# Rotary turning in a hybrid decoder trunk: one product and one sum of six operations put on GpSimd

## The chip, the core and the metric

The kernel runs on one core of a Trainium2 chip. The metric is the device time of one execution in microseconds (us). The engines are named as in the profile: PE (TensorE) multiplies matrices, DVE (VectorE) and ACT (ScalarE) work element by element, POOL (GpSimd) does a little arithmetic and issues a large part of the transfers, SP issues the loads of the weights.

## The reference, cut to what matters

Two layers are applied to 512 prompt positions and 8 sample positions at once, with a model width of 2048. Everything is in 32-bit floats.

```python
h = rmsnorm(x, norm_g)
z = h @ w_in                                   # 2048 x 8192
b_c, c_c, x_c, g_c, q, k, v, g_r = split_projection(z)
y_conv = b_c * short_conv(c_c * x_c) * silu(g_c)
q = rope(q.reshape(Bsz, L, 4, 256), pos)
k = rope(k.reshape(Bsz, L, 4, 256), pos) * 256 ** -0.5
o, new_S = retention(q, k, v, ret_S)           # four heads, chunks, state carried on
y_ret = groupnorm(o) * gn_g * silu(g_r)
x = x + concat(y_conv, y_ret) @ w_out
x = x + sigmoid(x @ w_pg) * (p_i @ w_ple)
```

`rope` splits each head of 256 into halves x1 and x2 and gives x1 cos - x2 sin and x1 sin + x2 cos: four products, one difference and one sum.

## The kernel before, in words

All activations lie with the features on the 128 partitions and the 520 positions (512 + 8) along the row, one slot of 128 x 520 floats for 128 features; there are 75 such slots in SBUF. A product of 2048 x 128 weights with all positions is computed twice over 260 columns (LEFT and RIGHT).

**Precision and the split.** Each float operand is cut into a high part and a remainder: ACT rounds to the high part (L229) and DVE subtracts it (L230). Each product is then three matmuls (L247 to L249): high by high, high by low, low by high. The weights come by SP's queue into a ring `raw` of 32 blocks of 128 x 128, and their parts go into a ring `split` of 60 blocks, from which PE reads. A block of a ring is free again only when its last reader is done.

**Pairs of products.** Two products at a time run through `pair`: for part of the depth (14 or 16 of the 16 blocks) by Strassen's method, which needs sums of weights, made by DVE in `raw` (L319), and the rest plainly. The finished halves are copied from PSUM to slots by ACT or added by DVE (L307 is the helper that records such operations with raised priority).

**A layer.** For each of four heads `retain(h)` takes q, k, v and the gate through `pair`. After q and after k it calls `rope`, copies the 8 sample positions to a small tile (`qks`, L830 and L839 on ACT), and stores the two turned slots to DRAM (`hs`, L815, a transfer issued by POOL). The chunks of retention are computed later, in nine steps (`steps`) that are put between the products of the next pairs; they fetch their pieces of q, k, v back from `hs` (L870, POOL). Then follow eight blocks of the convolution branch, the output product and the gate. Between pairs the states of the 8 samples are updated (`sample_step`): ACT scales (L777), DVE updates (L781) and reduces (L785), POOL loads and stores (L771, L772, L782).

**The turning.** `rope` has six operations on 128 x 520 slots. a and b are the two halves, rc and rs tables of cosine and sine that already hold the norm's factor, t1 and t2 fresh slots. L753 is t1 = a rc, L754 is t2 = a rs, L755 is a = b rs (it writes over a, so it must follow L753 and L754), L756 is t1 = t1 - a, L757 is b = b rc (after L755, which still reads b), and L758 is b = b + t2. There are 16 calls: q and k of four heads in two layers. In the profiled execution the calls of layer 0 lie between 69 and 345 us and those of layer 1 between 1117 and 1418 us.

**What sets the order.** The program is built by a framework whose scheduler, with a model of times of its own, sets for each engine one fixed order of instructions; each engine then works through its order without overtaking, and waits on semaphores where an operand is not ready. An instruction that waits therefore holds up everything behind it on its engine, POOL's transfers included.

Of the kernel before, what the change touches and what calls it, by code (L numbers as in the profile page):

```python
# [11 lines left out]
MUL, ADD, SUB = ALU.mult, ALU.add, ALU.subtract  # L12
# [67 lines left out]
class Slots:  # L80
# [8 lines left out]
    def get(self, dtype=F32):  # L89
        i = self.free.pop(0)  # L90
        self.count += 1
        t = self.pool.tile([P, T], dtype, tag=f"s{i}", name=f"slot{i}_{self.count}")
        self.used[id(t)] = (t, i)
        return t
# [4 lines left out]
    def put(self, *slots):  # L99
        for t in slots:  # L100
            self.free.append(self.used.pop(id(t))[1])
# [90 lines left out]
def trunk_kernel(  # L192
# [6 lines left out]
    V, S, G, PE, DMA = nc.vector, nc.scalar, nc.gpsimd, nc.tensor, nc.sync  # L199
# [516 lines left out]
    for l in range(DEPTH):  # L716
# [5 lines left out]
        def prepare():  # L722
            rc, rs = get(), get()
            SIDE.dma_start(rc, cosT)
            SIDE.dma_start(rs, sinT)
            with tc.high_priority():
                root = rms.root()
                rb = rms.spread(rms.diagonal(root))
                V.tensor_tensor(rc, rc, rb, MUL)
                V.tensor_tensor(rs, rs, rb, MUL)  # L730
            return root, rb, rc, rs

        def copied(ps):
            t = get()
            for n, v in zip((LEFT, RIGHT), ps):
                S.activation(t[:, n], v, AF.Copy)
            banks.put(*[v for v in ps if not any(v is o for o in over)])
            return Val(put, slot=t)
# [3 lines left out]
        root, rb, rc, rs = prepare()  # L742
# [6 lines left out]
        def rope(z0, z1):  # L749

            a, b = ((z if z.ps is None else copied(z.ps)).slot for z in (z0, z1))
            t1, t2 = get(), get()
            V.tensor_tensor(t1, a, rc, MUL)  # L753
            V.tensor_tensor(t2, a, rs, MUL)  # L754
            V.tensor_tensor(a, b, rs, MUL)  # L755
            V.tensor_tensor(t1, t1, a, SUB)  # L756
            V.tensor_tensor(b, b, rc, MUL)  # L757
            V.tensor_tensor(b, b, t2, ADD)  # L758
            put(a, t2)
            return [t1, b]  # L760

# [56 lines left out]
        def retain(h):  # L818
# [6 lines left out]
            if l == 0 and h == 0:  # L825
                q = rope(*first[:2])
            else:
                q = rope(*head(mt))
# [5 lines left out]
            if l == 0 and h == 0:  # L834
                kf = rope(*first[2:])
            else:
                kf = rope(*head(mt + 2))
# [641 lines left out]
```

## Time and profile before

| | |
|---|---|
| median of 3 runs | 2170.08 us (2166.74 to 2172.5) |
| profiled execution | 2172.46 us |
| its span | 2170.4 us, granted clock 0.998 |
| PE busy | 2148.5 us (99%), 17861 matmuls |
| DVE busy | 1895.7 us (87%) |
| ACT busy | 1266.2 us (58%) |
| POOL busy | 430.5 us (20%), 746 instructions |

The busy time of PE counts matmuls that overlap each other; whether PE runs at its pace is better read from the number of matmuls in equal stretches of time. "Idle before" and the view of waits name the instruction that ended a wait. "issue" is a wait for which the profile shows no cause.

### The profile page before, as it was taken

What the parts mean: (1) busy time and instruction counts of PE and PEld (TensorE: products, weight loads), DVE (VectorE), ACT (ScalarE), POOL (GpSimd) and SP (SyncE); (2) the same over time, 40 slices, a digit from 0 to 9 for tenths busy, and PEclk for the clock granted to TensorE, in tenths of its full rate; (3) what the DMA queues carried; (4) which work ended last, traced back from release to release, by engine and by line L of the source; (5) the groups of instructions that cost most, each with busy time, mean ns of one, the idle gap of its engine ahead of it and who ended that gap; (6) DMA issues with size and microseconds to landing.
All of it is one profiled execution on the core that took longest, in us unless ns stands there. A gap on an engine that the chain in (4) does not pass through costs nothing. (4 is left out here: it accounts for less than half of the span.)

```text
span 2170.4 us, 48198 instructions
## 1 busy us (share of the span) xinstructions
PE 2148.5 (99%) x17861; PEld 2142.9 (99%) x17861; DVE 1895.7 (87%) x3849; ACT 1266.2 (58%) x2661; POOL 430.5 (20%) x746
## 2 busy tenths in 40 slices
PE   9999999999999999999999999999999999999998
PEld 9999999999999999999999999999999999999998
DVE  8889989898999987987897988989999998878884
ACT  8656556655555555655765655565655555456565
POOL 2313222211001211210212222231111022121011
PEclk9999999999999999999999999999999999999999
DMA  8556675545543645645645566665464455566455
GB/s 288 176 169 196 185 215 183 186 152 172 156 134 120 228 156 186 217 153 161 214 144 174 172 210 193 190 195 183 147 182 145 127 155 199 181 212 195 127 169 192
DMA packets 182861, 387.31 MB, mean 178 GB/s; under 512 B 25888, under 2 KB 56352, under 8 KB 182624
## 3 DMA queue, kind: packets, MB, share of 16 engines
q1 hardware_dynamic: 129136, 213.77, 31.8%
q0 software_dynamic: 53056, 169.84, 23.8%
q8 instruction: 140, 2.29, 0.4%
q14 instruction: 97, 0.79, 0.1%
q10 hardware_dynamic: 432, 0.61, 0.1%
HBM read 318.96 MB, written 65.15 MB: 177 GB/s over the span
## 5 line engine op out<-in xcount | busy, mean ns | idle before, releaser
L247 PE MATMUL ps_g<-slot,split 128*128 128x260 f32 x5465 | 1532.3, 284 | 9.7 <-ACT slot L307 3.4
L248 PE MATMUL ps_g<-slot,split 128*128 128x260 f32 x5465 | 1535.1, 283 | 0.3 <-DVE slot L555 0.3
L249 PE MATMUL ps_g<-slot,split 128*128 128x260 f32 x5461 | 1520.5, 283 | 0.5 <-DVE split L230 0.5
L229 ACT ACTIVATE split<-raw 128x512 fp32r<-128x512 f32 (+2 forms) x1347 | 778.2, 596 | 587.6 <-DVE raw L319 205.6
L247 PEld LDWEIGHTS ps_g<-slot,split 128*128 128x128 f32 x5465 | 1024.5, 188 | 12.9 <-ACT slot L307 4.2
L248 PEld LDWEIGHTS ps_g<-slot,split 128*128 128x128 f32 x5465 | 1029.3, 188 | 0.5 <-DVE slot L555 0.5
L249 PEld LDWEIGHTS ps_g<-slot,split 128*128 128x128 f32 x5461 | 1020.3, 188 | 0.8 <-DVE split L230 0.7
L230 DVE TENSOR_TENSOR split<-raw,split 128x512 fp32r<-128x512 f32 (+2 forms) x1346 | 844.1, 647 | 176.5 <-PE ps_g L248 85.4
L319 DVE TENSOR_TENSOR raw<-raw 128x512 f32<-128x512 f32 (+1 forms) x660 | 426.2, 656 | 28.1 <-DMA raw<-wi 18.4
L307 ACT ACTIVATE slot<-ps_g 128x260 f32<-128x260 f32 x336 | 127.2, 381 | 142.5 <-PE ps_g L249 127.2
L551 ACT ACTIVATE slot<-slot 128x520 fp32r<-128x520 f32 (+1 forms) x212 | 109.1, 562 | 41.8 <-DVE slot L414 10.2
L552 DVE TENSOR_TENSOR slot<-slot,slot 128x520 fp32r<-128x520 f32 (+1 forms) x212 | 122.9, 609 | 4.3 <-ACT slot L551 4.2
L782 POOL DMA_DIRECT2D o_rets<-slot x64 | 35.3, 552 | 350.6 <-DVE slot L781 131.8
L307 DVE TENSOR_TENSOR slot<-ps_g,slot 128x260 f32<-128x260 f32 x168 | 70.5, 421 | 7.3 <-PE ps_g L249 4.9
L870 POOL DMA_DIRECT2D slot<-hs x64 | 46.1, 723 | 126.5 <-DVE split L230 35.5
L815 POOL DMA_DIRECT2D hs<-slot x64 | 35.6, 556 | 137.9 <-DVE slot L756 59.6
L747 DVE TENSOR_TENSOR slot<-slot,slot 128x520 f32<-128x520 f32 x80 | 55.4, 692 | 4.6 <-DMA o_rets<-slot 3.7
L1059 POOL DMA_DIRECT2D slot<-x1s x76 | 40.8, 538 | 88.0 <-PE ps_g L249 28.3
L781 DVE SCALAR_TENSOR_TENSOR slot<-slot,vs,slot 128x256 f32<-128x256 f32 x128 | 55.9, 477 | 2.6 <-ACT slot L777 2.3
L1209 POOL DMA_DIRECT2D x2s<-slot x30 | 16.3, 545 | 203.4 <-DVE slot L1204 202.5
L771 POOL DMA_DIRECT2D slot<-sret x64 | 35.5, 555 | 106.4 <-ACT split L229 43.4
L772 POOL DMA_DIRECT2D slot<-kq x64 | 34.9, 547 | 109.2 <-DVE slot L877 20.5
(217 smaller groups left out, 1727.0 us busy)
## 6 DMA issues: line engine op xcount, KB each, us to landing
raw<-wi SPq DMA_DIRECT2D x377, 256.0 KB, 3.9
raw<-wo SPq DMA_DIRECT2D x128, 256.0 KB, 5.6
raw<-wg SPq DMA_DIRECT2D x122, 256.0 KB, 4.2
raw<-wi SPq DMA_DIRECT2D x136, 192.0 KB, 4.0
slot<-x1s POOLq DMA_DIRECT2D x76, 260.0 KB, 5.0
slot<-sret POOLq DMA_DIRECT2D x64, 256.0 KB, 4.0
hs<-slot POOLq DMA_DIRECT2D x64, 256.0 KB, 3.9
slot<-hs POOLq DMA_DIRECT2D x64, 256.0 KB, 5.1
```

The source lines that it names most:

```text
L229: S.activation(hi, raw, AF.Copy)
L230: V.tensor_tensor(lo, raw, F(hi), SUB)
L247: PE.matmul(out, wh, xh, start=start, stop=False, skip_group_check=more)
L248: PE.matmul(out, wh, xl, start=False, stop=False, skip_group_check=more)
L249: PE.matmul(out, wl, xh, start=False, stop=stop, skip_group_check=more)
L307: fn(*args)
L319: V.tensor_tensor(out[:, n], x[:, n], y[:, n], op)
L551: keep(S.activation(hi, src[:, n], AF.Copy))
L552: V.tensor_tensor(lo, src[:, n], F(hi), SUB)
L747: V.tensor_tensor(out[:, n], v, table[:, n], MUL)
L781: keep(V.scalar_tensor_tensor(st[:, c], k, vs[:, h, e, b : b + 1], st[:, c], MUL, ADD))
L870: SIDE.dma_start(t[:, :512].rearrange("p (m n) -> p m n", m=2), src)
```

## The change

Two of the six operations of `rope` are given to POOL: the product a = b rs and the sum b = b + t2. The product b = b rc is moved up by one line, ahead of the difference.

```diff
             t1, t2 = get(), get()
             V.tensor_tensor(t1, a, rc, MUL)
             V.tensor_tensor(t2, a, rs, MUL)
-            V.tensor_tensor(a, b, rs, MUL)
+            G.tensor_tensor(a, b, rs, MUL)
+            V.tensor_tensor(b, b, rc, MUL)
             V.tensor_tensor(t1, t1, a, SUB)
-            V.tensor_tensor(b, b, rc, MUL)
-            V.tensor_tensor(b, b, t2, ADD)
+            G.tensor_tensor(b, b, t2, ADD)
             put(a, t2)
             return [t1, b]
```

The numbers of lines stay but their content shifts: now L755 is a = b rs on POOL, L756 is b = b rc and L757 is t1 = t1 - a, both on DVE, and L758 is b = b + t2 on POOL. L755 still has to wait until DVE has read a (L753, L754). L756 has to wait until POOL has read b, L757 until POOL has written a, and L758 until DVE has written b.

The scheduler makes a new order for each engine from this. It differs from the old one only in the stretches of the two layers in which heads are computed; in the convolution blocks, the output product, the gate and the tail every engine's order is the same as before.

First place: DVE, layer 1, the keys of the second head. Before:

```order
L999 SCALAR_TENSOR_TENSOR slot_894_15901<-ps_ot,vec,slot_894_15901 128x256 x2
L319 TENSOR_TENSOR raw<-raw 128x384 x2
L754 TENSOR_TENSOR slot_900_15918<-slot_879_15574,slot_808_14182 128x520
L755 TENSOR_TENSOR slot_879_15574<-slot_880_15575,slot_808_14182 128x520
L756 TENSOR_TENSOR slot_899_15917<-slot_899_15917,slot_879_15574 128x520
L757 TENSOR_TENSOR slot_880_15575<-slot_880_15575,slot_807_14181 128x520
L230 TENSOR_TENSOR split<-raw,split 128x512
L758 TENSOR_TENSOR slot_880_15575<-slot_880_15575,slot_900_15918 128x520
```

And now (879 is a, 880 is b, 899 and 900 are t1 and t2, 807 and 808 the tables):

```order
L999 SCALAR_TENSOR_TENSOR slot_894_15901<-ps_ot,vec,slot_894_15901 128x256 x2
L319 TENSOR_TENSOR raw<-raw 128x384
L754 TENSOR_TENSOR slot_900_15918<-slot_879_15574,slot_808_14182 128x520
L319 TENSOR_TENSOR raw<-raw 128x384
L756 TENSOR_TENSOR slot_880_15575<-slot_880_15575,slot_807_14181 128x520
L757 TENSOR_TENSOR slot_899_15917<-slot_899_15917,slot_879_15574 128x520
L230 TENSOR_TENSOR split<-raw,split 128x512
```

Between L754, which frees a for POOL, and L756, which needs POOL to be done with b, DVE has a single instruction. The keys of layer 0's second head stand the same way.

Second place: DVE, layer 1, the queries of the third head, as the other calls of `rope` stand. Now (927 is a, 928 is b, 934 and 935 are t1 and t2):

```order
L753 TENSOR_TENSOR slot_934_16830<-slot_927_16573,slot_807_14181 128x520
L754 TENSOR_TENSOR slot_935_16831<-slot_927_16573,slot_808_14182 128x520
L230 TENSOR_TENSOR split<-raw,split 128x512
L230 TENSOR_TENSOR split<-raw,split 128x384
L877 TENSOR_TENSOR slot_939_16968<-slot_930_16816,slot_938_16967 128x512
L319 TENSOR_TENSOR raw<-raw 128x512
L781 SCALAR_TENSOR_TENSOR slot_923_16553<-slot_924_16554,vs,slot_923_16553 128x256 x2
L230 TENSOR_TENSOR split<-raw,split 128x512
L230 TENSOR_TENSOR split<-raw,split 128x384
L756 TENSOR_TENSOR slot_928_16574<-slot_928_16574,slot_807_14181 128x520
L757 TENSOR_TENSOR slot_934_16830<-slot_934_16830,slot_927_16573 128x520
```

Eight other instructions of DVE stand between L754 and L756 here.

Third place: POOL around the same call, now:

```order
L1001 DMA ys<-slot_920_16384 128x2x256
L771 DMA slot_932_16826<-sret 128x512
L755 TENSOR_TENSOR slot_927_16573<-slot_928_16574,slot_808_14182 128x520
L782 DMA o_rets<-slot_923_16553 128x512
L758 TENSOR_TENSOR slot_928_16574<-slot_928_16574,slot_935_16831 128x520
L815 DMA hs<-slot_934_16830 128x512
L870 DMA slot_942_16975<-hs 128x2x256
L815 DMA hs<-slot_928_16574 128x512
```

The two operations are put into POOL's queue of transfers: the store of a sample's state (L782) stands between them, and the store of the turned slot that POOL itself finishes (928) behind them.

## The prediction

> **What bounds the kernel now.** I first read the page's shares, then the number of matmuls in stretches of 50 us, then the waits of PE and of DVE in the two stretches in which heads are computed.
>
> ```profile
> PE 2148.5 (99%) x17861; PEld 2142.9 (99%) x17861; DVE 1895.7 (87%) x3849; ACT 1266.2 (58%) x2661; POOL 430.5 (20%) x746
> ```
>
> PE is busy for 99% of the span, but DVE has 87%, so DVE could be what keeps PE from its pace in places. The view by stretches (columns: busy time and number of instructions of PE, PEld, DVE, ACT, POOL; then clock and transfers) tells where:
>
> ```profile
> 50.00:100.00 50.00, 49.97 (x413) 49.28 (x413) 44.15 (x89) 29.58 (x65) 15.06 (x26) 1.00 0.56 180
> 150.00:200.00 50.00, 50.00 (x421) 50.00 (x420) 43.81 (x101) 29.57 (x66) 16.90 (x30) 1.00 0.64 209
> 1100.00:1150.00 50.00, 49.60 (x410) 48.91 (x409) 42.84 (x87) 25.69 (x61) 12.60 (x19) 1.00 0.42 127
> 1250.00:1300.00 50.00, 49.10 (x412) 48.89 (x411) 44.37 (x102) 28.71 (x65) 12.09 (x21) 1.00 0.63 201
> 1350.00:1400.00 50.00, 49.79 (x415) 49.55 (x415) 43.09 (x98) 27.97 (x63) 12.49 (x22) 1.00 0.66 207
> 1450.00:1500.00 50.00, 49.19 (x408) 48.62 (x407) 45.95 (x106) 29.21 (x67) 12.40 (x21) 1.00 0.56 182
> 75.00:480.00 405.00, 404.97 (x3385) 404.76 (x3384) 365.18 (x796) 242.47 (x527) 106.70 (x184) 1.00 0.59 188
> 1125.00:1490.00 365.00, 363.08 (x3029) 361.95 (x3028) 320.99 (x707) 211.15 (x472) 94.91 (x164) 1.00 0.60 187
> ```
>
> A full stretch holds 420 or 421 matmuls, one each 50/420 = 0.119 us. Layer 0's heads (75 to 480 us) run at that pace, with 0.03 us of idle PE. Layer 1's (1125 to 1490) lose 8, 5 and 12 matmuls in three stretches, 25 x 0.119 = 3.0 us. The two stretches in which a layer's first turnings stand (50 to 100, 1100 to 1150) lack 7 and 10 more, 2.0 us together. So **all that a faster DVE could give back in the stages of the change is some 5 us**, 0.23% of the time. I take 0.3% (6.5 us) as the least that a measurement of this kernel can tell from no change.
>
> How near DVE is to being that limit, by its waits; the first two rows are of 75 to 480 us, the next two of 1125 to 1490 us, the last PE's longest of the latter:
>
> ```profile
> DVE split L230 <- PE ps_g L248: 10.0, 15, 1.5
> DVE split L230 <- ACT split L229: 8.2, 12, 1.2
> DVE split L230 <- ACT split L229: 16.1, 20, 2.7
> DVE raw L319 <- DMA raw<-wi: 13.4, 10, 3.1
> PE ps_g L247 <- ACT ps_g L307: 1.4, 2, 0.9
> ```
>
> In layer 0 DVE waits for PE to free blocks of the ring `split`: it is ahead by a full ring. In layer 1 there is no such row; DVE waits for the weights and for ACT instead. The ring is not full there, and a delay of DVE can come through to PE.
>
> **The change part by part.** *Taken from DVE:* two operations in each of 16 calls.
>
> ```profile
> L755 DVE TENSOR_TENSOR slot<-slot,slot 128x520 f32<-128x520 f32 x16 | 11.1, 691 | 0.0
> L758 DVE TENSOR_TENSOR slot<-slot,slot 128x520 f32<-128x520 f32 x16 | 11.0, 690 | 0.0
> ```
>
> That is 11.1 + 11.0 = 22.1 us of DVE, 11 us in each layer.
>
> *Put on POOL:* 32 operations of 520 columns. No row shows such an operation on POOL. What it has:
>
> ```profile
> L984 POOL TENSOR_TENSOR rstp<-rstd,half_neg 128x2 f32<-128x2 f32 x16 | 14.4, 900 | 20.1 <-DVE rstd L983 20.1
> L594 POOL MEMSET ones<- 128x128 f32 x1 | 0.2, 204 | 0.3 <-POOLq L1462 0.3
> L596 POOL MEMSET half_neg<- 128x32 f32 x1 | 0.1, 121 | 0.0
> ```
>
> The two fills give (204 - 121)/96 = 0.865 ns a column and 121 - 32 x 0.865 = 93 ns at the start, for one stream. 520 columns of one stream are 0.45 us. Three streams (two read, one written) one after the other are 0.093 + 3 x 0.45 = 1.44 us; DVE's own 0.69 us is the lower bound. A power is no guide to a product, so L984 (0.90 us for two columns) stays out. I take 1.2 us, the middle between two streams (0.99) and three, so 32 x 1.2 = 38 us on POOL, which is idle for four fifths of the span.
>
> *What the two engines do to each other.* The rows of POOL's longest operation and of DVE beside it, from the timelines:
>
> ```profile
> 673.17 5.83 POOL L1383 TENSOR_TENSOR rsn<-va,half_neg 128x32 f32<-128x32 f32 x1 [15.82 <-DVE va L1381]
> 673.00 0.69 DVE L319 TENSOR_TENSOR raw<-raw 128x512 f32<-128x512 f32 x1
> 674.76 0.69 DVE L230 TENSOR_TENSOR split<-raw,split 128x512 fp32r<-128x512 f32 x1 [1.07 <-issue]
> 675.48 0.69 DVE L319 TENSOR_TENSOR raw<-raw 128x512 f32<-128x512 f32 x1
> ```
>
> DVE stands for 1.07 us at the beginning of POOL's operation, with no cause that the profile shows, and then works on while POOL's still runs. The same comes at 1747 us (1.06). Over the whole trace such waits are few:
>
> ```profile
> DVE split L230 <- issue: 8.5, 16, 1.1
> ```
>
> 8.5/16 = 0.53 us each, and POOL's operations with two inputs are few too, 16 of them L984 with two columns. So POOL's reading holds DVE's up. One of 520 columns reads for longer. The bounds for one are 0 (DVE happens to work from PSUM or waits anyway) and 1.44 us (it stands for the whole); I take 1.0, the 1.07 of the row above. [...]
>
> *DVE's balance* is then 16 x (1.0 - 0.69) = +5 us a layer, with bounds of 16 x (0 - 0.69) = -11 and 16 x (1.44 - 0.69) = +12 us.
>
> *The new waits.* At the second heads' keys DVE has one L319 of 384 columns between L754 and L756; the trace of before has these, in that call of layer 1:
>
> ```profile
> 1233.09 0.70 DVE L754 TENSOR_TENSOR slot<-slot,slot 128x520 f32<-128x520 f32 x1 [1.10 <-DMA o_rets<-slot]
> 1233.82 0.70 DVE L755 TENSOR_TENSOR slot<-slot,slot 128x520 f32<-128x520 f32 x1
> 1234.56 0.70 DVE L756 TENSOR_TENSOR slot<-slot,slot 128x520 f32<-128x520 f32 x1
> 1237.00 0.55 DVE L230 TENSOR_TENSOR split<-raw,split 128x384 fp32r<-128x384 f32 x1
> ```
>
> 384 columns take 0.55 us, so DVE stands there for POOL's 1.2 - 0.55 = some 0.7 us, with the splits of weights behind it. One such call in each layer. At the other calls four to nine instructions stand between, some 4 x 0.55 = 2.2 us or more, which covers POOL's 1.2 and a standstill. Where that cover is gone, because POOL is late, the price is again up to 1.2 us a call. L758 is awaited by ACT (the copies L830, L839, ahead of splits L229) and by the store of the slot; ACT reaches the copy several splits later, as it did before. The transfers behind POOL's operations (L782, L815, L870, L771) go out up to 1.2 us later each. The stores of the heads waited already for DVE, 59.6 us in all, and their readers come a pair of products later:
>
> ```profile
> POOL hs L815 <- DVE slot L756: 59.6, 14, 17.2
> ```
>
> *What comes to PE.* In layer 0: nothing, because DVE's 10.0 us of waiting for a full ring take up the +5.0 + 0.7. In layer 1 DVE gets +5.7 us. How much of it is passed on, the trace says only roughly: there DVE waited 16.1 + 13.4 = 29.5 us for late inputs while PE lost 3.0, a tenth. That gives 0.6 us; if all of it came through, 5.7. I take 1 us, nearer to the row than to the bound. **The sum:** 2172.46 + 1 = 2173.5 us against the profiled execution, which lies 2.4 us above the median of the three runs; against that median 2170.1 + 1 = **2171 us**.
>
> **The rivals.** *Relief* (2167 us): POOL's reads fall into gaps, DVE keeps its 11 us a layer, and layer 1's three losses close: 2170 - 3.0. For it: at those losses DVE ran without a gap, and splits were late. Against: the 0.53 us rows, and that the waits in layer 1 are for weights on their way, which a faster DVE only asks for sooner. With the first turnings' 2.0 us as well it is 2165, still within 0.3%.
>
> *Standstill* (2179 us), on the other side: each of POOL's operations stops DVE for its whole length, and in layer 1, where no full ring stands between, DVE's delay goes to PE one to one. With 1.2 us that is 16 x 0.51 = 8.2, with the second head's 0.7 in all 8.9 us, so 2170.1 + 8.9; with 1.44 us it is 12.7 us, 2183. It decides from the point where DVE's net delay in layer 1 passed to PE exceeds 6.5 us, that is at a standstill of 0.69 + 5.8/16 = 1.05 us an operation if all is passed on. For it: most of DVE's rows have two inputs in SBUF (L230, L319). Against: DVE has 365 - 321 = 44 us of idle time in that stage to catch up in. [...]
>
> *The queue* (2174 us): POOL waits with L755 for DVE's L754 and the sample loads and stores behind it come late, so that ACT stands at L777 in front of splits. 8 calls of layer 1 by 0.5 us, one transfer's issue, is 4 us. Against: POOL is idle for 365 - 95 = 270 us of that stage, and its stores wait anyway.
>
> That the change does not do what it says is excluded by the order: both operations stand on POOL in all 16 calls.
>
> **How the numbers follow.** Likeliest (small net) 0.55, relief 0.20, standstill 0.20, the queue 0.05. Likeliest alone spans 2168 to 2175. The range reaches to relief's best and into the standstill: 2165 to 2181. Faster by over 0.3% would need all five us and a lucky run: 0.05. Slower by over 0.3% is the standstill, but for its weakest part, and a little of the others: 0.19. The rest, 0.76, is within 0.3%.
>
> **What would show it.** DVE's busy time falls by 22 us; POOL's L755 and L758 have 1.2 us (0.7 to 1.5) each; DVE's waits with no cause or with POOL as cause grow by some 32 us in all, beside L230 and L319; layer 0's stretches keep 420 matmuls; those of 1250 to 1500 us lack 25 to 40. Wrong I would be if layer 0 lost matmuls too (the ring is then no cover), if POOL's operations took over 2 us, or if layer 1 ran at 420 throughout.

## The result and the profile after

The changed kernel takes 2190.44 us in the median of 4 runs (2186.89 to 2194.2), beside 2168.77 us of the kernel before on the same chip: a ratio of 1.0098, with a 95% interval of 1.0075 to 1.0121. It is slower by 1%, some 21 us. The forecast was 2171 us, with a range that ended at 2181. A second comparison, within the last experiments, gave 1.0091 (1.0074 to 1.0108). The profiled execution has 2190.99 us and a span of 2189.2 us. All times of this document are of undisturbed executions; one execution of x10 below, the one that was profiled, was disturbed (9466.54 us) and is left out.

The page's first line, and the two stretches in which heads are computed, of the changed kernel (same columns as in the prediction):

```profile
PE 2154.2 (98%) x17861; PEld 2147.0 (98%) x17861; DVE 1907.6 (87%) x3817; ACT 1266.1 (58%) x2661; POOL 489.6 (22%) x778
75.00:480.00 405.00, 397.71 (x3292) 396.11 (x3291) 359.73 (x759) 230.75 (x509) 136.05 (x199) 1.00 0.58 184
1125.00:1490.00 365.00, 356.81 (x2958) 355.03 (x2957) 321.14 (x672) 207.83 (x461) 120.44 (x173) 1.00 0.57 183
```

DVE issues 32 instructions fewer (3817 against 3849) and is nevertheless busy for 11.9 us more. The first stretch holds 93 matmuls fewer than before, 11 us at 0.119 us each, the second 71 fewer, 8.4 us. Both layers lose; in a second execution of the changed kernel (x15 below) the two stretches lack 86 and 84.

**POOL's operations and what they do to DVE.** By lines, the four operations of the turning that were moved or shifted (busy us, mean ns of one, idle time before), of the changed kernel:

```profile
L755 POOL TENSOR_TENSOR slot<-slot,slot 128x520 f32<-128x520 f32 x16 | 35.9, 2244 | 51.9 <-DVE slot L754 29.6 <-ACT ps_g L307 12.7 <-DVE split L230 6.3
L758 POOL TENSOR_TENSOR slot<-slot,slot 128x520 f32<-128x520 f32 x16 | 25.7, 1607 | 14.9 <-DVE slot L756 14.7
L756 DVE TENSOR_TENSOR slot<-slot,slot 128x520 f32<-128x520 f32 x16 | 13.2, 828 | 4.8 <-POOL slot L755 4.8
L757 DVE TENSOR_TENSOR slot<-slot,slot 128x520 f32<-128x520 f32 x16 | 13.2, 826 | 0.0
```

One product on POOL takes 2.24 us in the mean, one sum 1.61. On DVE, L756 and L757, the instructions that were L757 and L756 before, grew from 0.69 to 0.83 us in the mean. The mean hides what happens; minimum, median and maximum of L755 and of L756 in ns, from the views of these lines, show it:

```profile
L755 POOL TENSOR_TENSOR slot<-slot,slot x16: 1290/1962/4791, 73.0 to 1425.0; 128x520 f32<-128x520 f32 x16
L756 DVE TENSOR_TENSOR slot<-slot,slot x16: 681/688/1796, 77.9 to 1429.7; 128x520 f32<-128x520 f32 x16
```

Most of DVE's instructions are untouched and a few are longer by some 1.1 us. The timeline of the first heads' turnings in layer 0 (start, duration, instruction, idle time before it) shows which, first on POOL, then on DVE (its first row holds two products, of 4.79 and 1.31 us):

```profile
73.04 6.06 POOL L755 TENSOR_TENSOR slot<-slot,slot 128x520 f32<-128x520 f32 x2 [2.29 <-DVE slot L754]
79.75 1.68 POOL L758 TENSOR_TENSOR slot<-slot,slot 128x520 f32<-128x520 f32 x1
82.49 1.32 POOL L758 TENSOR_TENSOR slot<-slot,slot 128x520 f32<-128x520 f32 x1
```

```profile
75.98 0.68 DVE L230 TENSOR_TENSOR split<-raw,split 128x512 fp32r<-128x512 f32 x1
77.87 1.79 DVE L756 TENSOR_TENSOR slot<-slot,slot 128x520 f32<-128x520 f32 x1 [1.20 <-POOL slot L755]
79.58 0.69 DVE L757 TENSOR_TENSOR slot<-slot,slot 128x520 f32<-128x520 f32 x1
80.19 1.80 DVE L756 TENSOR_TENSOR slot<-slot,slot 128x520 f32<-128x520 f32 x1
82.52 1.59 DVE L414 TENSOR_TENSOR slot<-slot,slot 128x260 f32<-128x260 f32 x1
```

First DVE works on and POOL's product needs 4.8 us. When DVE has to wait for it (1.20 us), POOL gets in, and from then on the two take turns: nearly each time that POOL works, one DVE instruction with two inputs in SBUF lasts 1.1 us longer, be it the turning's (1.79 and 1.80, with 0.69 for L757 between them) or another that stands there by chance (L414, 1.59 instead of the 0.42 that it had before). So the hold-up is no idle time of DVE but is counted as busy. Over the trace, this is so under 28 of POOL's 32 operations: one DVE instruction lasts longer than is usual for its kind, by 0.56 to 1.47 us, 1.06 us in the mean and 29.7 us in all. DVE's busy time says nearly the same. With the order of the changed kernel, but only 8 columns for each of POOL's operations (x1 below), DVE is busy for 1880.2 us; the 1907.6 us of the change are 27.4 us more, 0.86 us for each of the 32 operations. That the two operations taken away relieve DVE's busy time by only 1895.7 - 1880.2 = 15.5 us, and not by the 22.1 us of their rows, is because DVE's instructions overlap in the profile (the durations of all in the kernel before add up to 2164.3 us) and busy time counts an overlap once. The 28 longer instructions all take two operands from SBUF (15 are L230, 5 L781, two each L319, L756 and L757, one each L414 and L785). Four that take one from PSUM began and ended while POOL was at such an operation, and kept their times (L919 at 250.76, 1331.02 and 1335.90 us, 0.47 us each; L999 at 1400.80 us, 0.48). Under POOL's other four operations no instruction is longer; they are the four products that DVE waited for, 1.20 to 1.21 us each.

L414 in the kernel before:

```profile
77.46 0.42 DVE L414 TENSOR_TENSOR slot<-slot,slot 128x260 f32<-128x260 f32 x1
```

**From DVE to PE.** By lines, the first matmul of each product of three, before and after (number, busy us, mean ns, idle before it and its causes); the first row is of the kernel before, the second of the changed kernel:

```profile
L247 PE MATMUL ps_g<-slot,split 128*128 128x260 f32 x5465 | 1532.3, 284 | 9.7 <-ACT slot L307 3.4 <-ACT ps_g L307 2.9 <-ACT split L229 1.9
```

```profile
L247 PE MATMUL ps_g<-slot,split 128*128 128x260 f32 x5465 | 1536.2, 284 | 22.8 <-ACT slot L307 12.1 <-ACT ps_g L307 4.9 <-ACT split L229 2.5
```

PE's waits for split weights hardly grew (1.9 to 2.5 us). What grew are its waits for ACT's copies of finished halves out of PSUM (L307), from 6.3 to 17.0 us. ACT is idle for two fifths of the time; its copies are late because ACT works in order and, mostly, stands ahead of them for something else. The same stretch, on ACT and then on PE:

```profile
80.36 0.21 ACT L830 ACTIVATE qks<-slot 128x8 f32<-128x8 f32 x1 [1.63 <-DVE slot L757]
82.63 0.21 ACT L839 ACTIVATE qks<-slot 128x8 f32<-128x8 f32 x1 [1.79 <-DVE slot L757]
84.14 1.32 ACT L551 ACTIVATE slot<-slot 128x520 fp32r<-128x520 f32 x2 [0.41 <-DVE slot L414]
85.97 0.36 ACT L307 ACTIVATE ps_g<-ps_g 128x260 f32<-128x260 f32 x1
```

```profile
86.39 0.39 PE L247 MATMUL ps_g<-slot,split 128*128 128x260 f32 x1 [2.82 <-ACT ps_g L307]
```

DVE's late L757 holds ACT up twice at the copies of the sample positions, its late L414 once more, and the copy that PE needs comes at 85.97 us; PE stood for 2.82 us. In layer 1 another wait stands at the head of ACT's queue, for DVE's sum of raw weights, which waited for its load:

```profile
1414.31 0.56 DVE L319 TENSOR_TENSOR raw<-raw 128x384 f32<-128x384 f32 x1 [3.23 <-DMA raw<-wi]
1414.90 0.52 ACT L229 ACTIVATE split<-raw 128x384 fp32r<-128x384 f32 x1 [4.22 <-DVE raw L319]
1415.33 0.37 ACT L307 ACTIVATE slot<-ps_g 128x260 f32<-128x260 f32 x1
1415.75 0.39 PE L247 MATMUL ps_g<-slot,split 128*128 128x260 f32 x1 [1.32 <-ACT slot L307]
```

Ten stalls of PE of over 0.4 us lie in the two stretches of the changed kernel, 14.6 us in all. Ahead of six of them (8.6 us) ACT had stood for DVE, as in these two. Ahead of three (3.8 us) ACT had stood for a slot that a transfer of POOL's queue had not yet released, and in one (2.2 us) PE waited for DVE itself. One of the three, behind which PE stood for 1.47 us:

```profile
314.57 0.39 ACT L307 ACTIVATE slot<-ps_g 128x260 f32<-128x260 f32 x1 [3.84 <-DMA hs<-slot]
```

**Where the time is lost.** PE's new order differs from the old one only within the stretches of heads (at least 1680 of the 17861 places hold a matmul of another line or tile) and has as many matmuls, so the matmul at each place of the order can be compared with the one at the same place before. This is how much later than before it comes, in us; the columns are moments of the kernel before, the rows single profiled executions (x-names are the experiments below):

```
                       100    200    300    500   1100   1150   1300   1500   1700   2175
the change             5.9    6.4    9.2   11.7    9.8   13.4   13.9   17.6   18.3   19.8
the change again, x15  3.9    4.4    7.6    9.1   10.1   14.0   14.3   20.9   21.4   23.0
x1  cut to 8 columns   0.2    0.3    0.3    0.9    0.5    0.5   -0.7   -1.9   -1.6   -0.4
x6  hold-up alone      6.4    6.2    9.7   11.1    8.9    9.4   11.2   13.2   12.9   12.8
x13 products whole     0.6    0.7    1.9    1.6    0.9    1.4    2.4    4.2    4.8    6.1
x14 sums whole         1.1    1.2    1.2    1.1   -1.4   -1.4   -2.4    0.0    0.6    1.7
```

The time goes in a few steps of 1 to 4 us, the first within the first two turnings, and little is lost outside the two stretches of heads. The two executions of the change differ by up to 3.3 us from each other, so smaller differences in this table say little.

### The profile page after: what moved, and what is told of

Read it like the earlier page. It is cut to its first block, busy times and chain, and to the rows that moved or that the text cites. A ratio compares the mean times of both kernels' runs of the same rounds, so it can differ in the third digit from the quotient of the medians.

```text
span 2189.2 us, 48241 instructions
## 1 busy us (share of the span) xinstructions
PE 2154.2 (98%) x17861; PEld 2147.0 (98%) x17861; DVE 1907.6 (87%) x3817; ACT 1266.1 (58%) x2661; POOL 489.6 (22%) x778
## 3 DMA queue, kind: packets, MB, share of 16 engines
q0 software_dynamic: 53056, 169.84, 23.7%
## 5 line engine op out<-in xcount | busy, mean ns | idle before, releaser
L230 DVE TENSOR_TENSOR split<-raw,split 128x512 fp32r<-128x512 f32 (+2 forms) x1346 | 859.2, 658 | 170.4 <-PE ps_g L248 84.7
L319 DVE TENSOR_TENSOR raw<-raw 128x512 f32<-128x512 f32 (+1 forms) x660 | 427.4, 658 | 40.3 <-DMA raw<-wi 33.5
L307 ACT ACTIVATE slot<-ps_g 128x260 f32<-128x260 f32 x336 | 126.5, 380 | 119.0 <-PE ps_g L249 102.6
L782 POOL DMA_DIRECT2D o_rets<-slot x64 | 35.4, 553 | 351.8 <-DVE slot L781 137.9
L307 DVE TENSOR_TENSOR slot<-ps_g,slot 128x260 f32<-128x260 f32 x168 | 70.5, 420 | 3.1 <-PE ps_g L249 1.7
L781 DVE SCALAR_TENSOR_TENSOR slot<-slot,vs,slot 128x256 f32<-128x256 f32 x128 | 60.6, 514 | 7.3 <-ACT slot L777 7.2
L1141 POOL DMA_DIRECT2D x1s<-slot x32 | 17.4, 545 | 184.6 <-DVE slot L1139 184.6
```

What stands on the lines that cost most here:

```text
L230: V.tensor_tensor(lo, raw, F(hi), SUB)
L307: fn(*args)
L319: V.tensor_tensor(out[:, n], x[:, n], y[:, n], op)
L781: keep(V.scalar_tensor_tensor(st[:, c], k, vs[:, h, e, b : b + 1], st[:, c], MUL, ADD))
```

## The experiments

Where an experiment says "the order of the changed kernel" (or of before), every engine's order was kept as it was and only the instructions named were exchanged, so that the scheduler had no part in it; the diffs of these runs name instructions and not lines of the source. The kernel before, run beside each of the four groups (x1 to x4, x5 to x8, x9 to x12, x13 to x16), had 2170.91, 2170.65, 2168.89 and 2170.37 us.

**Is it the new order, or the reading?** x1 keeps the order and the relief of DVE and takes nearly all of POOL's work away; x2 keeps POOL at work without reading.

```diff
 order of the changed kernel
-POOL L755, L758  TENSOR_TENSOR 128x520   x32
+POOL L755, L758  TENSOR_TENSOR 128x8     x32     (x1)
+POOL L755, L758  MEMSET 128x520          x32     (x2)
```

> The changed program with its orders of instructions kept to the row, only the 32 operations that POOL got work on 8 columns instead of 520 (the products and sums of the other 512 columns are left out, so the turned queries and keys are wrong). Hold-up theory (POOL's reading of SBUF stops one instruction of DVE for about 1.1 us each time): the loss goes with POOL's reading, and DVE keeps the 22 us it was relieved of: 2165 to 2172 us, no DVE instruction of 512 columns near 1.8 us. Order theory (the scheduler's new order is itself worse): it stays at 2185 us or above. Waiting theory (DVE, ACT and the transfers behind wait for a slow POOL): it falls as well, since POOL is done in some 0.3 us; this run does not tell it from the hold-up.

> The changed program, orders and waits kept to the row, but each of the 32 operations of POOL is a fill of the same 520 columns: it writes and reads nothing (the product a = b rs and the sum are replaced by a constant). About 0.55 us each by the row of the fills before, instead of a median of 1.7 to 2.0. Hold-up theory: without reads no DVE instruction is stretched, 2165 to 2173 us. Waiting theory: POOL still makes DVE wait, for a third to a half as long, so a third to a half of the 20 us stays: 2176 to 2181 us. Order theory: 2185 us or above.

x1 took 2170.53 us (ratio 1.0007, 0.9997 to 1.0017), x2 2171.32 us (1.0004, 0.9994 to 1.0014). In x2 DVE's instructions are not longer, as the view of L756 shows (ns); L230, L319 and L781 have the means of the kernel before as well (647, 656 and 477 ns):

```profile
L756 DVE TENSOR_TENSOR slot<-slot,slot x16: 686/692/700, 75.1 to 1410.7; 128x520 f32<-128x520 f32 x16
```

So neither the order nor POOL's queue costs anything, and the loss needs POOL's reading. These two also measure what the relief of DVE is worth: nothing that can be seen, with DVE's busy time at 1880 us.

**The hold-up alone, without the relief.** In the order of before, 32 products of 520 columns on a spare tile, which nobody waits for, ahead of the stores of the turned slots (x3), and the same with fills (x4).

```diff
 order of the kernel before
+POOL TENSOR_TENSOR spare<-spare,spare 128x520    x32     (x3)
+POOL MEMSET spare 128x520                        x32     (x4)
 POOL L815  DMA hs<-slot
```

> The kernel before, every engine's order kept, with 32 more operations on POOL, each just ahead of the store of a turned slot: a product of a spare 520-column tile with itself, for which no other engine waits. DVE is not relieved of anything. Hold-up theory: 32 times some 1.1 us of DVE without the 22 us of relief, so slower than the change: 2190 to 2205 us, with one DVE instruction of about 1.8 us under nearly each of POOL's. Order theory and waiting theory: POOL's extra work delays only its own transfers by 1.3 us each: within 4 us of the kernel before.

> As the run with the extra products, but the 32 extra operations are fills of the spare tile, which read nothing (about 0.55 us each). Hold-up theory: within 3 us of the kernel before, DVE's 512-column instructions at 0.68 us. If POOL's transfers being late is what counts, some of the loss of the run with products shows here too: 3 to 10 us slower than before.

x3 took 2181.66 us (1.0052, 1.0037 to 1.0067), x4 2167.56 us (0.9986, 0.9977 to 0.9996). Here reading costs time and writing doesn't. But x3 missed its expectation: with the hold-up and without the relief it should have cost at least as much as the change, and it cost half. Its DVE was busy 23.7 us longer than before, in the page's first line:

```profile
PE 2152.9 (99%) x17861; PEld 2146.5 (98%) x17861; DVE 1919.4 (88%) x3849; ACT 1263.6 (58%) x2661; POOL 489.6 (22%) x780
```

A theory that counts DVE's time alone falls here: DVE is busy for 11.8 us longer than in the change, and PE loses half as much.

**The waits alone, and the hold-up alone, at the places of the change.** x5 has three fills in the place of each operation, so that POOL is at work for 1.6 us each time, and what waits for it has to wait, without the hold-up. x6 has the operations cut to 8 columns, which is what others wait for, and behind each a whole product on a spare tile.

```diff
 order of the changed kernel
-POOL L755, L758  TENSOR_TENSOR 128x520   x32
+POOL L755, L758  MEMSET 128x520 three times  x32                           (x5)
+POOL L755, L758  TENSOR_TENSOR 128x8, then spare<-spare,spare 128x520  x32 (x6)
```

> The order of the changed kernel; in place of each of POOL's 32 operations stand three fills of the same 520 columns, one after the other, the first with the operation's wait and the last with its signal. A fill took 0.53 to 0.56 us and stretched no instruction of DVE in the run with one fill, so three are 1.6 to 1.8 us: the time of the changed kernel's operation (median 1.7 to 2.0) with all that waits for it, but without the hold-up of DVE. Not computed: the product and the sum (the outputs that depend on them are other values). Theory 'hold-up' (the whole loss of 20 us comes from the stretched instructions of DVE): 2168 to 2174 us, since the waits alone cost nothing. Rival 'waits' (half of the loss comes from DVE and ACT waiting for POOL's slow result, the other half from the hold-up): 2176 to 2183 us, with DVE waiting for POOL at L756 or L757.

> The order of the changed kernel; POOL's 32 operations are cut to 8 columns (their results are awaited as in the changed kernel), and behind each stands a product of 520 columns on a spare tile, for which nobody waits but POOL's own queue. Not computed: 512 columns of each product and sum. It has the hold-up of DVE at the places of the change and the relief of 22 us, but not the waits for a slow result. Theory 'hold-up': 2186 to 2193 us, as the change. Rival 'waits': 2175 to 2183 us, like the order of before with 32 such products (2181.7), or less by the relief.

x5 took 2170.46 us (1.0001, 0.9992 to 1.0011): waits of this size alone cost nothing. They are about half of those of the change, though, because nothing holds the fills up: DVE waited for the products for 2.7 us (4.8 in the change) and ACT at its copies of the sample positions (L830, L839) for 9.8 us (23.0 in the change). x6 took 2181.58 us (1.0053, 1.0038 to 1.0068): the hold-up at the places of the change, with the relief, costs half of the change's loss. The hold-up is there, with DVE busy for 1906.0 us (1907.6 in the change), though each reading product stands a little later than in the change. In lines of x6:

```profile
L1359 POOL TENSOR_TENSOR spare<-spare 128x520 f32<-128x520 f32 x32 | 42.8, 1337 | 0.0
L756 DVE TENSOR_TENSOR slot<-slot,slot 128x520 f32<-128x520 f32 x16 | 15.2, 952 | 0.4
```

So theory "hold-up" is refuted as the whole cause, and "waits" as well in the form that a result that comes 1.6 us late costs by itself. What is left is that waits cost on top of the hold-up; waits as long as the change's, but without a hold-up, were not tried. The table above shows where: by 500 us x6 has lost 11.1 us, as much as the change (11.7 and 9.1), but between 1100 and 1500 us it loses 4.3 us and the change 7.8 and 10.8. In these single executions the hold-up alone makes up the loss of layer 0, and what the waits add lies in layer 1.

**One operation alone, in the scheduler's own order.** Both kernels keep b = b rc at the place that it has in the change.

```diff
-            V.tensor_tensor(a, b, rs, MUL)
+            G.tensor_tensor(a, b, rs, MUL)     # x7: the sum stays on DVE
-            V.tensor_tensor(b, b, t2, ADD)
+            G.tensor_tensor(b, b, t2, ADD)     # x8: the product stays on DVE
```

> Only the product a = b rs goes to POOL (16 operations), the sum stays on DVE, with the order that the scheduler makes for that. Theory 'hold-up': half of the operations, half of the loss, 2177 to 2183 us. Rival 'waits': the product is what DVE itself waits for (L756 and L757), so it has most of the loss, 2182 to 2190 us.

> Only the sum b = b + t2 goes to POOL (16 operations), the product stays on DVE, with the order that the scheduler makes for that. Theory 'hold-up': half of the loss, 2177 to 2183 us. Rival 'waits': nothing of DVE waits for the sum, only ACT's copies of the samples and the stores do, so 2170 to 2177 us.

x7 took 2179.12 us (1.0040, 1.0025 to 1.0055), x8 2182.76 us (1.0059, 1.0042 to 1.0076). The sum, for which nothing on DVE waits, costs no less than the product. Both lost nearly all in layer 1 (69 and 91 matmuls of the stretch 1125 to 1490 us) and little in layer 0 (14 and 11). These kernels have orders of their own, so the sum of the two (1.0%) proves nothing about the change; x13 and x14 repeat the question in its order.

**ACT's copies of the samples.** In x9 the copies L830 and L839 read a constant and wait for nothing.

```diff
 order of the changed kernel
-ACT L830, L839  ACTIVATE qks<-slot 128x8      x32
+ACT L830, L839  ACTIVATE spare<-ones 128x8    x32, 31 of them without a wait
```

> The order of the changed kernel, with POOL's 32 operations whole; ACT's 32 copies of the sample positions (L830, L839, 8 columns each) read a constant and write a spare tile, so that 31 of them wait for nothing; the waits that later instructions of ACT need move to the first of these that uses the slots of that turning. Not computed: the sample positions of q and k for the samples' states. In the changed kernel ACT stood 22.8 us at these copies, ahead of splits of weights, against 10.2 us in the order of the change with the products on a spare tile (2181.6 us). Theory 'copies' (the 9 us that the change costs beyond the hold-up of DVE are ACT standing at the copies until DVE and POOL are done): 2179 to 2184 us. Rival 'DVE alone' (ACT only waits for what is late anyway; the other 9 us are DVE's own, at L756 and L757): 2187 to 2192 us.

It took 2186.86 us (1.0079, 1.0064 to 1.0094), between the two expectations. Against the kernel before beside it that is a loss of 18.0 us, where the change lost 21.7 and, as x15 below, 20.7. The interval overlaps both of those, so it is not shown that freeing ACT at these places gives anything back.

**Half a hold-up.**

```diff
 order of the changed kernel
-POOL L755, L758  TENSOR_TENSOR 128x520   x32
+POOL L755, L758  TENSOR_TENSOR 128x260   x32
```

> The order of the changed kernel, POOL's 32 operations cut from 520 to 260 columns. Not computed: half of each product and sum. POOL's operation is then some 0.7 us uncontended, and the hold-up of DVE some 0.5 us instead of 1.1, against a relief of 0.69 an operation. Theory 'in proportion' (half the hold-up costs half of the 20 us): 2178 to 2183 us. Rival 'slack first' (PE loses only what goes beyond the relief and the ring's slack): 2170 to 2175 us.

It took 2176.86 us in the median of four (1.0032, 1.0017 to 1.0046), between the expectations again: a third of the loss of the change for half of the columns.

**More blocks of raw weights.** The stall at 1414 us begins with a late load, so a longer ring `raw` was to take the loss away.

```diff
-RAW = 32
+RAW = 40
-SPLIT = 60
+SPLIT = 52
```

> The kernel before with 40 blocks of raw weights instead of 32 and 52 split blocks instead of 60 (the same memory); the scheduler makes a new order on every engine. It is the base for the run with the same rings and the change. 2160 to 2185 us, since the order is another one.

> The changed kernel with 40 raw and 52 split blocks. Theory 'raw ring' (DVE's delay reaches PE because the 32 raw blocks come free late and the next load takes some 4 us): 8 blocks more are 2 loads of 4 blocks ahead, so that the change costs under 8 us against the kernel before with the same rings. Rival 'split ring or nothing of the kind': it costs 15 us or more, as with 32.

Without the change 2183.27 us (1.0066, 1.0049 to 1.0083), with it 2199.26 us (1.0139, 1.0123 to 1.0154): the change costs 16.0 us with these rings as well. That the raw ring is what lets DVE's delay through is refuted, as far as an experiment can that shortens the other ring and has another order.

**One operation whole in the order of the change, and DVE's waits taken away.** x13 keeps the products whole and cuts the sums to 8 columns, x14 the reverse; x16 has whole sums, and for the products what x6 has; x15 is the change again.

```diff
 order of the changed kernel
-POOL L758  TENSOR_TENSOR 128x520   x16
+POOL L758  TENSOR_TENSOR 128x8     x16                                     (x13)
-POOL L755  TENSOR_TENSOR 128x520   x16
+POOL L755  TENSOR_TENSOR 128x8     x16                                     (x14)
+POOL L755  TENSOR_TENSOR 128x8, then spare<-spare,spare 128x520   x16      (x16)
```

> The order of the changed kernel; POOL's 16 products (L755) whole, its 16 sums (L758) cut to 8 columns. Not computed: 512 columns of each sum. Theory 'shares' (11 us from the hold-up of DVE whoever waits, half of it from each operation; some 5 us from DVE's waits for the product; some 3.5 us from ACT's copies): 5.5 + 5, so 2178 to 2183 us. Rival 'together' (PE loses only where the hold-ups of both operations fall together and the slack is used up): under 2176 us here and in the run with the sums whole.

> The order of the changed kernel; POOL's 16 sums (L758) whole, its 16 products (L755) cut to 8 columns. Not computed: 512 columns of each product. Theory 'shares': 5.5 us of hold-up and some 3.5 us by ACT's copies of the samples, so 2176 to 2181 us. Rival 'together': under 2176 us.

> The changed kernel itself, beside the others of this call: 2187 to 2193 us by both theories.

> The order of the changed kernel; POOL's 16 sums whole; its 16 products cut to 8 columns (awaited by DVE as before), and behind each a product of 520 columns on a spare tile, for which only POOL's queue waits. Not computed: 512 columns of each product. The hold-up of all 32 operations stays and ACT's copies wait for whole sums, but DVE doesn't wait for a slow product. Theory 'shares': the change less DVE's waits, 2183 to 2187 us. Rival 'together': the hold-ups fall as in the change, 2187 to 2192 us.

x13 took 2175.53 us (1.0026, 1.0015 to 1.0036), x14 2175.88 us (1.0027, 1.0017 to 1.0036), x15 2191.02 us (1.0091, 1.0074 to 1.0108), x16 2186.81 us (1.0072, 1.0057 to 1.0087). The halves cost 0.26% and 0.27%, 0.53% together; the whole costs 0.91%. The halves don't add up to the whole (with their intervals 0.32 to 0.72% together, against 0.74 to 1.08%), and that speaks for "together"; that each half has the whole relief doesn't explain it, for the relief alone is worth nothing (x1). The table above shows where it comes from: by 500 us, the end of layer 0's heads, x13 and x14 have lost 1.6 and 1.1 us, the change 9 to 12. x16 lies at the border of the two expectations. By the medians, taking DVE's waits for the product away gives back 4.2 us, but the interval overlaps that of x15, so this isn't shown.

None of these kernels is faster than the one before by the 0.3% that the prediction took for the least change to be told (the nearest is x4, by 0.14%), and x1 says why moving these two operations would not have helped: the whole relief, with next to nothing paid for it, gains nothing.

## Why the prediction was wrong, step by step

**What bounds the kernel and what DVE could gain**: right, with some 5 us as an upper bound. With the order and the relief of the change and next to no reading (x1), nothing is gained: the ratio is 1.0007 (0.9997 to 1.0017).

**The operations on POOL**: 1.2 us was taken, within 0.69 to 1.44. The shortest took 1.29 us. The means of 2.24 and 1.61 us contain what the text had only for DVE: POOL is held off by DVE too, up to 4.8 us in all. That is one of the text's own signs of being wrong ("if POOL's operations took over 2 us").

**The hold-up of DVE**: 1.0 us an operation was taken, from one row of 1.07; measured are 1.06 us in the mean of the 28 longer instructions, and 0.86 us of busy time an operation. The relief was taken as 0.69 us an operation and is 0.48 (15.5 us in 32). As both were taken too large by about as much, the balance of DVE (+5 us a layer) came out right: its busy time rose by 11.9 us, 6 a layer. But the hold-up was looked for in the wrong place. The text expected DVE's busy time to fall by 22 us and its waits without a cause, or for POOL, to grow by some 32 us. Those for POOL grew by the 4.8 us below, and those without a cause, 8.5 us before, didn't grow:

```profile
DVE split L230 <- issue: 6.2, 16, 1.1
```

**The new waits**: too few. DVE waits for the product in 4 places, 4.8 us (1.4 were taken), and ACT waits for 23.0 us at its copies of the samples (7.4 before). In the size that they have in x5 they cost nothing when taken alone.

**What comes to PE**: this is the step that failed. It had two halves. "In layer 0: nothing, because DVE's 10.0 us of waiting for a full ring take up" the delay: layer 0 lost 9 to 12 us, about as much as layer 1 (8 to 11). The text had named this as a sign of being wrong ("if layer 0 lost matmuls too"). "A tenth" in layer 1: there 5.7 us of delay on DVE became a loss greater than that. Two things were missed:

- A full ring of split weights covers PE only against late splits. PE was not short of splits, as the waits above show; it stood for ACT's copies out of PSUM, mostly behind ACT's waits for DVE, and the ring `split` doesn't lie on that way. The cover was even there: in layer 0 of the changed kernel, from 75 to 480 us, DVE still waits for a full ring (the row below: us, times, longest), while PE loses 11 us. That this is the way is read from the waits of the traces; no experiment took ACT's copies out of their queue, and what x9 gave back, which freed ACT at one kind of wait only, is within the intervals. What cover there is, is finite: x13 and x14 show that layer 0 takes up the hold-up of one operation in each of its 8 calls nearly whole, with 1.1 to 1.6 us of loss, and x6 that it doesn't take up that of both (11.1 us).

```profile
DVE split L230 <- PE ps_g L248: 7.3, 9, 1.7
```

- The delay was spread evenly over a layer in the sum, 5 us in 365. It comes in lumps: a wait of 1.20 us and three instructions longer by 1.1 us each within 8 us at the first turnings. The relief of the same turnings, two operations of 0.69 us in each of two calls, is 2.8 us. DVE's idle time in the two stages (40 and 44 us in the kernel before) is for the most part elsewhere.

So the loss has two parts. The hold-up of all 32 operations, less the relief, costs 0.53% (x6), and nothing is left of it without reads (x1, x2, x5). The rest, from 0.53 to 0.91%, comes when the results are also awaited; the intervals of x6 and x15 don't overlap. How it is divided between DVE's waits for the product (x16), ACT's for the turned slots (x9) and the late transfers of POOL's queue stays open: what x16 and x9 give back is within the intervals, and no run separates the transfers.

**The rivals**: "Standstill" came nearest: it held that the hold-up exceeds the relief and that all of the delay is passed on to PE. It was given 0.20 and priced for layer 1 alone, 8.9 us; layer 1 lost 8 to 11. That its price fits is in part luck, for it took the hold-up as 1.2 us an operation and the way as late splits. With the same price in layer 0, which it left out, it would have come to 2170 + 18 = 2188. "Relief" is refuted by x1. "The queue" costs nothing by itself (x2, x4 and x5); the three stalls behind late transfers, 3.8 us, show that it can take part where the hold-up is.

## What to carry to other kernels

A row that shows how long one engine holds up another is worth little until one knows what the delayed engine's own customers have queued behind it: look at what is next on each in-order queue, not only at the ring between two engines. Price a delay by the few microseconds in which it falls, not by its mean over a stage; two halves of a change can cost more together than their sum, 0.91% against 0.53% here, when each alone still finds slack. And here, with DVE busy for 87% of the span, an operation handed to GpSimd that reads SBUF was not simply taken off DVE: each took 0.48 us of DVE's busy time off and put 0.86 us on.

## What the runs showed that was not expected

**PE's clock after a stall.** The stretches around the stall at 83 us, and one in layer 1 behind a stall of 2.1 us (counted from the start of one matmul to the start of the next; the number before the transfers' share is the granted clock):

```profile
83.20:86.30 3.10, 0.37 (x4) 0.16 (x2) 3.10 (x7) 2.65 (x7) 2.97 (x6) 1.00 0.73 210
87.80:91.20 3.40, 3.40 (x18) 3.40 (x17) 1.82 (x4) 2.06 (x5) 2.69 (x6) 0.51 0.93 315
91.20:95.00 3.80, 3.80 (x34) 3.80 (x34) 1.94 (x5) 1.13 (x3) 1.24 (x2) 1.00 1.06 393
1159.60:1163.00 3.40, 3.40 (x18) 3.40 (x17) 3.33 (x9) 1.52 (x3) 1.11 (x2) 0.51 0.46 153
```

After the stall PE runs for some 3.3 us at half its clock, about 15 matmuls at 0.217 us instead of 0.119, which is another 1.5 us. In the change's trace this came three times, from 9.36, 87.88 and 1159.51 us (granted clock 0.51 each time), after stalls of 2.27, 3.10 and 2.12 us; two more, of 2.24 us at 738 us and of 2.52 us at 1329 us, were not followed by it. In the trace of before it came once, from 729.73 us (0.50), after a stall of 2.23 us. Why it comes after some stalls and not after others is not shown.

**Reading, not working, is what disturbs.** 32 fills of 520 columns on POOL (0.53 to 0.56 us each) lengthened none of DVE's instructions in the views (x2: L756 0.700 us at most, L230 0.647 us in the mean, as before), and neither did 96 (x5: 0.702 and 0.647 us). Products of 8 columns, which do read, took 0.97 us each in the mean on POOL in x1 (L755), the first two 3.84 us together, and beside them DVE's instructions kept their times as well (L756 0.700 us at most, L230 0.647 us in the mean): there it is POOL that is late, and this costs no time (ratio 1.0007).
